# The input projection of a hybrid decoder block, whole and first, as seven block products per column pair

## The chip, the cores and the metric

One core of a Trainium2 chip runs the kernel. The metric is the device time of one execution in microseconds (us). Of the kernel before there are three timed runs, and one further execution that the hardware profiler recorded. The engines are named as the profile names them: PE is TensorE (PEld its weight loads), DVE is VectorE, ACT is ScalarE, POOL is GpSimd, SP is SyncE, which only issues DMAs here.

## What is computed

One layer over x of 1024 rows and 1024 columns, all in float32.

```python
u = rms_norm(h, mix_pre_g)
z = jnp.einsum('bsd,de->bse', u, w_in)      # 1024 x 4096
p, q, k, v = z[..., :o1], z[..., o1:o2], z[..., o2:o3], z[..., o3:o4]   # 512 columns each
gate_a, gate_b = z[..., o4:o5], z[..., o5:]                             # 1024 columns each
ya = jnp.einsum('bsc,cd->bsd', pool_mixer(p, pool_mix, pool_scale), w_branch_a)
yb = jnp.einsum('bsc,cd->bsd', diff_attention(q, k, v, ...), w_branch_b)
m = jax.nn.sigmoid(gate_a) * ya + jax.nn.sigmoid(gate_b) * yb
h = h + rms_norm(jnp.einsum('bsd,de->bse', m, w_out), mix_post_g)
u = rms_norm(h, ffn_pre_g)
f = jax.nn.silu(u @ w_ffn_gate) * (u @ w_ffn_up)
h = h + rms_norm(f @ w_ffn_down, ffn_post_g)
```

pool_mixer takes causal window means of 2, 4, 8 and 16 rows less the row itself, one window for each of four groups of 128 columns, and multiplies each group by its own 128 x 128 matrix. diff_attention has four heads with two 64-wide query and key parts each; a head's weights are the softmax of the first part less lambda times that of the second, with a linear distance bias and a causal mask.

## The kernel before

Every matrix product is made of float32r matmuls: each operand is split into a high part (a copy rounded to float32r, on ACT) and a low part (the rest, a subtraction on DVE), and three matmuls of 128 x 128 by 512 columns are summed: high by high, high by low, low by high. mac (line 103) does that for a plain product. Activations lie transposed, features on partitions.

The program is one traced function. A planner puts each engine's instructions in order from its own estimate of costs: among those whose inputs it holds to be ready, the earliest in program order goes first. Each engine then runs its queue strictly in that order, and so does each DMA queue. A pool of tiles is shared by tag: a8 has 16 buffers of 8 KB per partition, b4 has 14 of 4 KB, the weight tags wraw, whi and wlo have two of 4 KB each; in PSUM the tags mm, fil and pair have two buffers each (pair is two banks). A tile waits until a buffer of its tag is free. Code under tc.manual_schedule, or in tc.keep_in_program_order, keeps its written order on the engines named.

The stages, in program order:
- Start (first_block, line 208, and norm_steps, line 133): eight blocks of 128 rows of x are loaded, normed, transposed and split into uT (eight a8 buffers). Head 0's q and k products run in half-width pieces (proj_steps, line 190) as the blocks become ready.
- Attention (scores, transposes, values, from line 284): 32 blocks of four heads, in the order QORDER within a head, three in flight (AHEAD). Each block has scores on PE, a reduction on DVE that adds the bias and finds the row maximum, the exponential on ACT, a combination on DVE, transposes on PE, copies and subtractions (AT), the value matmuls on PE, and scalings on ACT and DVE. Beside it a filler generator is advanced by PACE steps for each attention step: head_proj (line 229) of the next head, the pool's projection (pool_windows, line 366) beside head 3.
- Pool mixing (from line 466), then the gated branches: gated (line 490) makes, for each of eight column blocks and two halves, the plain gate product (24 matmuls), the branch product (12 matmuls), the sigmoid on ACT and the multiplication on DVE; first for branch a, then for branch b with the transposed attention output (OT).
- Output projection and second norm (out_matmul, line 587), which keep the normed rows as quadrants of a two by two block matrix.
- FFN gate and up (gate_up, line 698): each pair of a gate and an up column block is a two by two block product, made with seven block products instead of eight: 7 x 4 x 3 = 84 matmuls for 96. ffn_weights builds the weight sums, sums and convert_u2 the activation sums S1 to S4.
- FFN down, also with seven products, operands through DRAM (fsd), and the last norm.

The projection of w_in has 32 column blocks of 128: four each for p, q, k and v, eight for each gate. Each costs 2 halves x 8 x 3 = 48 matmuls.

## Time and profile before

| | |
|---|---|
| median of three runs | 1319.32 us (1318.79 to 1319.73) |
| the profiled execution, its own time | 1322.02 us |
| span of the profiled execution, first to last instruction | 1320.2 us |
| mean granted TensorE clock in it | 0.996 |
| PE, DVE, ACT, POOL busy | 1292.2, 753.5, 528.9, 125.4 us |
| DMA | 128.81 MB, mean 98 GB/s |

The span is what the rows lie in; the execution's own time is 1.8 us longer, and 2.7 us above the median of the other runs. The busy time of an engine is the union of its instructions in a stretch. A matmul's duration runs from its start to its modelled end and overlaps the next one's, so the cost of a stream of matmuls is read from the distance of starts. A row of groups (by line) has the sum of one line's instructions, their mean in ns, and the engine's idle time just before them with what ended it.

### The profile page before, as it was taken

The page shows a single profiled execution, that of the slowest core. Times are in us where ns is not written, and L with a number is a line of the kernel's source. Part 1 is how long each engine was busy: PE and PEld are TensorE (multiplying, and loading weights), DVE is VectorE, ACT ScalarE, POOL GpSimd, SP SyncE. Part 2 cuts the span into 40 slices and gives each one's busy share as a digit, 9 for nine tenths or more (in the row PEclk, how much of TensorE's full clock was granted, in tenths as well). Part 3 has the DMA queues.
Part 4 walks back from the last instruction along what each step waited for, and adds up shares of the span by engine and source line. Part 5 has one row for each costly group of instructions (what it writes and reads, how often), then busy time and mean ns, then how long its engine had stood idle before and what let it go on. Part 6 is the DMA issues. An engine that isn't in the chain of part 4 may idle for free.

```text
span 1320.2 us, 15626 instructions
## 1 busy us (share of the span) xinstructions
PE 1292.2 (98%) x6024; PEld 1069.6 (81%) x6024; DVE 753.5 (57%) x1182; ACT 528.9 (40%) x967; POOL 125.4 (9%) x112
## 2 busy tenths in 40 slices
PE   5899999999999999999999999999999999999997
PEld 5788888887888788878878888888888888888886
DVE  5366676876111322255579756555655536874666
ACT  5256565545111211144455333333333324454552
POOL 4000000000000000001010111111101111000222
PEclk9899999999999999999999999999999999999999
DMA  6221212001111211143332323323232348833235
GB/s 211 65 53 44 65 33 64 9 25 40 44 45 44 78 48 48 48 144 112 116 124 71 110 99 120 120 97 104 88 112 95 105 165 284 276 105 103 88 104 199
DMA packets 123738, 128.81 MB, mean 98 GB/s; under 512 B 6288, under 2 KB 92816, under 8 KB 122256
## 3 DMA queue, kind: packets, MB, share of 16 engines
q1 hardware_dynamic: 120112, 121.39, 29.2%
q10 hardware_dynamic: 3552, 6.43, 1.3%
q8 instruction: 47, 0.77, 0.2%
q14 instruction: 27, 0.22, 0.0%
HBM read 95.03 MB, written 28.57 MB: 94 GB/s over the span
## 4 chain that ended last, share of the span: by engine, by line
PE 90%; DVE 4%; DMA 2%; ACT 1%; issue 1%; POOL 1%; SPq 0%; DVEq 0%; ACTq 0%; POOLq 0%
PE Y L688 6%; PE Y L689 6%; PE Y L687 6%; PE gate L109 4%; PE gate L111 4%; PE gate L110 4%; PE X L687 3%; PE X L689 3%; PE X L688 3%; PE o L344 3%; PE Yd L688 2%; PE Yd L689 2%; PE Yd L687 2%; PE branch L111 2%; PE branch L109 2%; PE branch L110 2%
## 5 line engine op out<-in xcount | busy, mean ns | idle before, releaser
L109 PE MATMUL gate<-uTh,wg_hi 128*128 128x512 f32 x256 | 101.5, 397 | 0.8 <-ACT p L376 0.4
L110 PE MATMUL gate<-uTl,wg_hi 128*128 128x512 f32 x256 | 101.3, 396 | 0.0
L111 PE MATMUL gate<-uTh,wg_lo 128*128 128x512 f32 x256 | 101.3, 396 | 0.0
L87 DVE TENSOR_TENSOR w_op<-wd,w_op 128x512 fp32r<-128x512 f32 x77 | 56.3, 731 | 50.1 <-ACT w_op L624 50.1
L624 ACT CAST w_op<-wd 128x512 fp32r<-128x512 f32 x77 | 47.9, 622 | 74.7 <-PE Yd L689 31.5
L629 DVE TENSOR_TENSOR p<-Z,p 128x512 f32<-128x512 f32 x21 | 14.5, 691 | 106.1 <-PE Z L689 106.1
L688 PE MATMUL Y<-A_lo,Wh 128*128 128x512 f32 x184 | 71.7, 390 | 0.3 <-DVE A_lo L87 0.3
L689 PE MATMUL Y<-A_hi,Wl 128*128 128x512 f32 x184 | 71.6, 389 | 0.0
L687 PE MATMUL Y<-A_hi,Wh 128*128 128x512 f32 x184 | 71.6, 389 | 0.0
L655 ACT CAST Wh<-wf_t 128x1024 fp32r<-128x1024 f32 x42 | 44.1, 1051 | 66.1 <-PE X L688 30.1
L127 POOL TENSOR_TENSOR rstd<-ms,mhalf 128x1 f32<-128x1 f32 (+1 forms) x11 | 11.7, 1064 | 603.7 <-DVE ms L126 587.5
L688 PE MATMUL Yd<-w_op,s_op 128*128 128x512 f32 x176 | 68.7, 390 | 0.2 <-DVE w_op L87 0.2
L687 PE MATMUL Yd<-w_op,s_op 128*128 128x512 f32 x176 | 68.6, 390 | 0.0
L689 PE MATMUL Yd<-w_op,s_op 128*128 128x512 f32 x176 | 68.3, 389 | 0.0
L309 ACT ACTIVATE E<-E,nm 128x1024 f32<-128x1024 f32 (+7 forms) x64 | 49.5, 774 | 40.3 <-DVE nm L306 39.8
L687 PE MATMUL X<-S_hi,Wh 128*128 128x512 f32 x168 | 65.4, 389 | 0.0
L688 PE MATMUL X<-S_lo,Wh 128*128 128x512 f32 x168 | 65.4, 389 | 0.0
L689 PE MATMUL X<-S_hi,Wl 128*128 128x512 f32 x168 | 65.4, 389 | 0.0
L687 PE MATMUL Y<-S_hi,Wh 128*128 128x512 f32 x168 | 65.4, 389 | 0.0
L688 PE MATMUL Y<-S_lo,Wh 128*128 128x512 f32 x168 | 65.4, 389 | 0.0
L689 PE MATMUL Y<-S_hi,Wl 128*128 128x512 f32 x168 | 65.4, 389 | 0.0
L87 DVE TENSOR_TENSOR wg_lo<-wg_raw,wg_hi 128x1024 fp32r<-128x1024 f32 x16 | 19.6, 1225 | 76.0 <-ACT wg_hi L101 76.0
(271 smaller groups left out, 3430.2 us busy)
## 6 DMA issues: line engine op xcount, KB each, us to landing
s_raw<-fsd SPq DMA_DIRECT2D x35, 512.0 KB, 3.6
wf_raw<-in_w_ffn_gate_dram SPq DMA_DIRECT2D x22, 512.0 KB, 3.7
wf_raw<-in_w_ffn_up_dram SPq DMA_DIRECT2D x22, 512.0 KB, 3.8
fsd<-fss SPq DMA_DIRECT2D x11, 1024.0 KB, 3.8
wd<-in_w_ffn_down_dram SPq DMA_DIRECT2D x44, 256.0 KB, 5.6
fsd<-F SPq DMA_DIRECT2D x33, 256.0 KB, 2.3
wg_raw<-in_w_in_dram SPq DMA_DIRECT2D x16, 512.0 KB, 3.9
xt<-in_x_dram SPq DMA_DIRECT2D x8, 512.0 KB, 8.1
```

The lines of the kernel that those rows point to most:

```text
L87: nc.vector.tensor_tensor(out=o, in0=a, in1=f32(hi), op=ALU.subtract)
L109: nc.tensor.matmul(o, ah, bh, start=i == 0, stop=False)
L110: nc.tensor.matmul(o, ah, bl, start=False, stop=False)
L111: nc.tensor.matmul(o, al, bh, start=False, stop=i == n - 1)
L309: nc.scalar.activation(E[m], E[m], AF.Exp, bias=nm[:, m:m + 1], scale=-1.0, accum_out=sums[:, m:m + 1])
L344: nc.tensor.matmul(o, ats[b // 4][:, j, b % 4 * P:(b % 4 + 1) * P], V[:, b, :, :], start=b == 0 and j == 0, stop=b == qb and j == 1)
L624: nc.scalar.copy(hi, a)
L629: nc.vector.tensor_tensor(out=o, in0=a, in1=b, op=op)
L655: nc.scalar.copy(hi, a)
L687: nc.tensor.matmul(o, ah, bh, start=start, stop=False, skip_group_check=goes_on)
L688: nc.tensor.matmul(o, ah, bl, start=False, stop=False, skip_group_check=goes_on)
L689: nc.tensor.matmul(o, al, bh, start=False, stop=stop, skip_group_check=goes_on)
```

## The change

The whole input projection comes first. Heads 0 and 1 have their q and k made plainly as before (common); the other 28 column blocks form 14 pairs, each made by seven block products in seven_steps, the routine that gate_up now shares: q with k of heads 2 and 3, v with a pool group (vp_unit, four of them), gate a with gate b (eight). The results go to DRAM: q and k in high and low parts (qkd), v transposed and split (vd), the pool branch's mixed output (yd), the sigmoids of the gates (sgd). load_head reads a head back into QA, QB, K and V.

The x norm runs in a written order on ACT, DVE and POOL, with the first weights' low parts on POOL; in its second half it also builds the raw sums for S1 to S4. The units follow. Of the last gate pair's 28 steps, 4 are taken before attention is begun, and the other 24 are the first of the filler. The filler then loads the pool output, head 1, and computes branch a (64 steps of three matmuls), with its weights' low parts on POOL instead of DVE. PACES sets the steps taken for each attention step: 2.2 for the first 9 steps, 0.5 for the next 10, then 0.3. Heads 2 and 3 are loaded during the head before. Branch b runs after attention. What follows (the output projection on) is the same work; some helpers have moved and been renamed.

```diff
 A8, B4 = 16, 14
-GROUPS = [2] * 9 + [4]
 QORDER = (7, 0, 6, 1, 5, 2, 4, 3)
-LAG, LAG_P = 4, 12
-PACE = (0.8, 0.8, 0.8, 0.7)
+LAG = 4
+PACES = (2.2, 0.5, 0.3, 0.3)
...
+    def load_w(src, k, n, s, pool=False):
 
         raw = wp.tile([P, k, n], F32, tag="wraw", bufs=2, name=name(s + "_raw"))
         hi = wp.tile([P, k, n], F32R, tag="whi", bufs=2, name=name(s + "_hi"))
         lo = wp.tile([P, k, n], F32R, tag="wlo", bufs=2, name=name(s + "_lo"))
         nc.sync.dma_start(raw, src.rearrange("(k p) n -> p k n", p=P))
-        if start:
-            tc.keep_in_program_order(nc.scalar.copy(hi, raw))
-            for i in range(0, k, 2):
-                tc.keep_in_program_order(nc.gpsimd.tensor_tensor(
-                    out=lo[:, i:i + 2, :], in0=raw[:, i:i + 2, :], in1=f32(hi[:, i:i + 2, :]), op=ALU.subtract))
+        nc.scalar.copy(hi, raw)
+        if pool:
+            nc.gpsimd.tensor_tensor(out=lo, in0=raw, in1=f32(hi), op=ALU.subtract)
         else:
-            nc.scalar.copy(hi, raw)
             sub(lo, raw, hi)
...
+        g, u = raw_weights(first, "wraw"), raw_weights(second, "whi")
+        operand(g, "B11", "B21")
+        t13, t24 = (wp.tile([P, 2, 4, P], F32, tag="wlo", bufs=2, name=name("wf_t")) for _ in range(2))
+        tt(t13[:, 0], u[:, 0], g[:, 0], ALU.subtract)
+        tt(t13[:, 1], u[:, 1], u[:, 0], ALU.subtract)
+        operand(t13, "T1", "T3")
+        tt(t24[:, 0], u[:, 1], t13[:, 0], ALU.subtract)
+        tt(t24[:, 1], g[:, 1], t24[:, 0], ALU.subtract)
+        operand(t24, "T2", "T4")
+        operand(u[:, 1:], "B22")
+        return W
...
+        yield from product_steps(Y, W["B11"], U["A11"], True)
+        p1 = temp("p1")
+        nc.scalar.copy(p1, Y)
+        yield from product_steps(X, W["T1"], U["S1"], True)
+        p5 = temp("p5")
+        nc.scalar.copy(p5, X)
+        yield from product_steps(Y, W["T2"], U["S2"], False)
+        u2 = temp("u2")
+        nc.scalar.copy(u2, Y)
+        yield from product_steps(Z, W["B21"], U["A12"], True)
+        add(Z, p1, 0, 0)
+        yield from product_steps(Y, W["T3"], U["S3"], False)
+        add(Y, p5, 1, 1)
+        yield from product_steps(X, W["B22"], U["S4"], False)
+        add(X, u2, 1, 0)
+        yield from product_steps(Y, W["T4"], U["A22"], False)
+        done(0, 1, Y)
...
+    U = {n: operand(n) for n in ("A11", "A12", "A21", "A22")}
+    traws = {n: a8([P, 4, HALF], F32, n + "_raw") for n in ("A11", "A12", "S1", "S3")}
+    traws["S2"], traws["S4"] = traws["A11"], traws["A12"]
...
+    qkd = [[dr.tile([P, 2, S], F32, name=name("qkd")) for _ in range(2)] for _ in range(NH)]
+    vd = [dr.tile([P, 2, S], F32, name=name("vd")) for _ in range(NH)]
+    yd = [dr.tile([P, 2, S], F32, name=name("yd")) for _ in range(4)]
+    sgd = [[dr.tile([P, S], F32, name=name("sgd")) for _ in range(KD)] for _ in range(2)]
...
+    def qk_done(h, e, t, src, st=None):
+        st = b4([P, 2, HALF], F32R, "qk_st") if st is None else st[e][:, :, half(t)]
+        hi, lo = st[:, 0], st[:, 1]
+        if e == 0:
+            qs = 1.0 / (8.0 * 0.25 ** (h + 1))
+            nc.scalar.mul(hi, src, qs)
+            nc.vector.scalar_tensor_tensor(out=lo, in0=src, scalar=qs, in1=f32(hi), op0=ALU.mult, op1=ALU.subtract)
+        else:
+            split((hi, lo), src)
+        nc.scalar.dma_start(qkd[h][e][:, :, half(t)], f32(st))
...
+    with tc.manual_schedule(engines={nc.scalar.engine, nc.vector.engine, nc.gpsimd.engine}):
+        for tb in range(2):
+            square(tb)
+            rstd(tb)
+        for tb in range(2):
+            normed(tb)
+        first_hi(0)
+        for part in range(4):
+            first_lo(0, part)
+        square(2)
+        rstd(2)
+        o = [(fil("q"), fil("k")), (mm("q"), mm("k"))]
+
+        def first_pair(i):
+            for e in range(2):
+                common(0, e, i // 2, o[i // 2][e], slice(i % 2 * 2 * P, (i % 2 + 1) * 2 * P))
+
+        for tb in range(NB):
+            t, cols = tb // 4, slice(tb % 4 * P, (tb % 4 + 1) * P)
+            both = pair("x_t")
+            for k in range(KD):
+                nc.tensor.transpose(both[:, k // 4, k % 4 * P:(k % 4 + 1) * P], xts[tb][:, k * P:(k + 1) * P], ident)
+            v = [both[:, kq, :].rearrange("p (k t) -> p k t", k=4) for kq in range(2)]
+            ops = [[a[:, :, cols] for a in U[f"A{t + 1}{kq + 1}"]] for kq in range(2)]
+            for kq in range(2):
+                nc.scalar.copy(ops[kq][0], v[kq])
+            if tb + 3 < NB:
+                square(tb + 3)
+            if tb in (0, 2, 4):
+                first_hi(tb // 2 + 1)
+            for kq in range(2):
+                sub(ops[kq][1], v[kq], ops[kq][0])
+            if tb + 2 < NB:
+                normed(tb + 2)
+            if tb + 3 < NB:
+                rstd(tb + 3)
+            if tb < 6:
+                for part in range(2):
+                    first_lo(tb // 2 + 1, part + tb % 2 * 2)
+            if t == 0:
+                for kq in range(2):
+                    nc.scalar.copy(traws[f"A1{kq + 1}"][:, :, cols], v[kq])
+            else:
+                s1, s2, s3, s4 = (traws[f"S{i + 1}"][:, :, cols] for i in range(4))
+                nc.scalar.copy(s1, v[0])
+                tt(s1, v[1], s1, ALU.add)
+                tt(s2, s1, s2, ALU.subtract)
+                tt(s3, v[1], s2, ALU.subtract)
+                tt(s4, s4, s2, ALU.subtract)
+            if tb + 5 < NB:
+                xts.append(load_x(tb + 5))
+            if tb < 2:
+                first_raw(tb + 2)
+            if tb in (3, 5, 7):
+                first_pair(tb // 2 - 1)
+            if tb == 7:
+                for e in range(2):
+                    qk_done(0, e, 0, o[0][e])
+    first_pair(3)
+    for e in range(2):
+        qk_done(0, e, 1, o[1][e])
+    W = weights(w_cols(o_q, 2), w_cols(o_k, 2))
+    for t in range(2):
+        o = (fil("q"), fil("k")) if t == 0 else (mm("q"), mm("k"))
+        for e in range(2):
+            common(1, e, t, o[e], slice(0, HALF))
+            qk_done(1, e, t, o[e])
+    for n in ("S1", "S2", "S3", "S4"):
+        U[n] = operand(n)
+        split(U[n], traws[n])
...
+    def vp_unit(h):
+
+        VS = a8([P, 2, S], F32R, "v_st")
+        v = VS.rearrange("p i (b d) -> p b i d", b=NB)
+        pp = a8([P, 2, S], F32, "p")
+        p, seen = pp[:, 0, :], [0, 0]
+
+        def done(e, t, src):
+            seen[e] += 1
+            if e == 0:
+                if t == 1:
+                    vt = temp("vt")
+                    nc.scalar.copy(vt, src)
+                    src = vt
+                pt = fil("vT")
+                for i in range(4):
+                    nc.tensor.transpose(pt[:, i * P:(i + 1) * P], src[:, i * P:(i + 1) * P], ident)
+                pt = pt.rearrange("p (b d) -> p b d", b=4)
+                split((v[:, t * 4:t * 4 + 4, 0, :], v[:, t * 4:t * 4 + 4, 1, :]), pt)
+                if seen[e] == 2:
+                    nc.scalar.dma_start(vd[h], f32(VS))
+            elif seen[e] == 2:
+                later.append(lambda: pool(h, p, pp[:, 1, :]))
+
+        unit(w_cols(o_v, h), w_cols(0, h), done, lambda e, t: p[:, half(t)] if e == 1 else None)
...
+        tmp = [s0, b4([P, S], F32, "s")]
+        win = WINDOWS[g]
+        s, w, i = p, 1, 0
+        while w < win:
+            s2 = tmp[i]
+            nc.vector.tensor_copy(s2[:, :w], s[:, :w])
+            tt(s2[:, w:], s[:, w:], s[:, :S - w], ALU.add)
+            s, w, i = s2, 2 * w, 1 - i
+        tt(s[:, :16], s[:, :16], cnt[:, g, :], ALU.mult)
+        tt(p[:, :16], s[:, :16], p[:, :16], ALU.subtract)
+        nc.vector.scalar_tensor_tensor(out=p[:, 16:], in0=s[:, 16:], scalar=1.0 / win, in1=p[:, 16:],
+                                       op0=ALU.mult, op1=ALU.subtract)
+        y = b4([P, S], F32R, "yh"), b4([P, S], F32R, "yl")
+        split(y, p)
+        o = pair("y")
+        for t in range(2):
+            mac(o[:, t, :], [((pm[:, 0], pm[:, 1]), tuple(a[:, half(t)] for a in y))])
+        o = o.rearrange("p t c -> p (t c)")
+        y2 = b4([P, S], F32R, "y2h"), b4([P, S], F32R, "y2l")
+        nc.scalar.mul(y2[0], o, psc[:, g:g + 1])
+        nc.vector.scalar_tensor_tensor(out=y2[1], in0=o, scalar=psc[:, g:g + 1], in1=f32(y2[0]),
+                                       op0=ALU.mult, op1=ALU.subtract)
+        for i in range(2):
+            nc.scalar.dma_start(yd[g][:, i, :], f32(y2[i]))
...
+    def gate_done(d):
+        st, seen = [b4([P, S], F32, "g_st") for _ in range(2)], [0, 0]
+
+        def done(e, t, src):
+            nc.scalar.activation(st[e][:, half(t)], src, AF.Sigmoid)
+            seen[e] += 1
+            if seen[e] == 2:
+                nc.scalar.dma_start(sgd[e][d], st[e])
+        return done
+
+    def unit(first, second, done, where=lambda e, t: None, W=None):
+        W = W or weights(first, second)
+        while later:
+            later.pop(0)()
+        seven(W, U, done, where)
+
+    for h in range(2, NH):
+        unit(w_cols(o_q, h), w_cols(o_k, h),
+             W=W if h == 2 else None, done=partial(qk_done, h, st=[a8([P, 2, S], F32R, "qk_st") for _ in range(2)]))
+    for h in reversed(range(NH)):
+        vp_unit(h)
...
+    def load_head(h):
+
+        QA, K = (a8([P, 2, S], F32R, n) for n in ("QA", "K"))
+        for m in range(2):
+            r, r2 = hs[m], hs[1 - m]
+            nc.sync.dma_start(f32(K[r, m, :]), qkd[h][1][r, 0, :])
+            nc.sync.dma_start(f32(K[r2, m, :]), qkd[h][1][r, 1, :])
+            for rr in (r, r2):
+                nc.sync.dma_start(f32(QA[rr, m, :]), qkd[h][0][r, 0, :])
         yield
+        QB, V = (a8([P, 2, S], F32R, n) for n in ("QB", "V"))
+        for m in range(2):
+            for rr in hs:
+                nc.sync.dma_start(f32(QB[rr, m, :]), qkd[h][0][hs[m], 1, :])
+        nc.sync.dma_start(f32(V), vd[h])
+        heads[h] = QA, QB, K, V.rearrange("p i (b d) -> p b i d", b=NB)
+
+    head0 = load_head(0)
+    for d in range(KD - 1):
+        if d == 3:
+            next(head0)
+        unit(w_cols(o_ga, d), w_cols(o_gb, d), gate_done(d))
+
+    last_unit = seven_steps(weights(w_cols(o_ga, KD - 1), w_cols(o_gb, KD - 1)), U, gate_done(KD - 1))
+    for _ in range(4):
+        next(last_unit)
+    for _ in head0:
+        pass
...
+    def branch(e, w, mov, take):
+
+        for d in range(KD):
+            bh, bl = load_w(w[:, d * P:(d + 1) * P], 4, P, "wb", e == 0)
+            for t in range(2):
+                sg = temp(("p1", "sg")[t])
+                nc.sync.dma_start(sg, sgd[e][d][:, half(t)])
+                o = fil("branch")
+                for k in range(4):
+                    triple(o, bh[:, k, :], bl[:, k, :], *mov(t, k), k == 0, k == 3, False)
+                    yield
+                take(d, t, o, sg)
...
+    def filling():
+        yield from last_unit
+        for i in range(2):
+            y2.append((a8([P, 2, S], F32R, "y2h"), a8([P, 2, S], F32R, "y2l")))
+            for j in range(2):
+                for t, s in zip(y2[i], range(2)):
+                    nc.sync.dma_start(f32(t[:, j, :]), yd[2 * i + j][:, s, :])
+        ma.extend([[a8([P, 4, HALF], F32, "ma") for _ in range(KD // 4)] for _ in range(2)])
+        for _ in load_head(1):
+            pass
+        yield from branch(0, w_branch_a, quad_mov(y2), take_a)
+
+    filler = filling()
...
-            owed += pace
-            while filler is not None and owed >= 1.0:
+            owed += PACES[min(steps // 10, len(PACES) - 1)]
+            while owed >= 1.0:
                 owed -= 1.0
-                if next(filler, True):
-                    owed = -1e9
+                next(filler, None)
...
+            if pos == 2 and 0 < h < NH - 1:
+                for _ in load_head(h + 1):
+                    pass
             step(scores(*seq[j]))
```

## Rows read from the trace of the kernel before

**Rows 1.** Page, part 1: busy us, share of the span, instructions.

```profile
PE 1292.2 (98%) x6024; PEld 1069.6 (81%) x6024; DVE 753.5 (57%) x1182; ACT 528.9 (40%) x967; POOL 125.4 (9%) x112
```

**Rows 2.** Busy time by stretch: attention, gated branches, FFN gate and up.

```profile
core 0: us, PE busy (x) PEld busy (x) DVE busy (x) ACT busy (x) POOL busy (x), PEclk, DMA share, GB/s
76.90:297.00 220.10, 220.10 (x1199) 188.96 (x1198) 160.08 (x363) 123.15 (x308) 5.96 (x3) 1.00 0.16 41
316.00:582.70 266.70, 266.70 (x1161) 214.65 (x1160) 73.08 (x94) 54.64 (x79) 0.00 (x0) 1.00 0.19 57
706.10:1086.90 380.80, 380.80 (x1681) 315.31 (x1680) 227.26 (x264) 134.58 (x181) 63.11 (x41) 1.00 0.33 108
```

**Rows 3.** ACT in order of time: start, us, what; first copy of two FFN units.

```profile
744.23 0.59 ACT L707 COPY p<-Y 128x512 f32<-128x512 f32 x1 [1.44 <-issue]
763.26 0.59 ACT L707 COPY p<-Y 128x512 f32<-128x512 f32 x1 [1.45 <-issue]
```

**Rows 4.** ACT in order of time: sigmoids of two gate column blocks, one half.

```profile
480.03 0.59 ACT L501 ACTIVATE sg<-gate 128x512 f32<-128x512 f32 x1
496.83 0.59 ACT L501 ACTIVATE sg<-gate 128x512 f32<-128x512 f32 x1
```

**Rows 5.** Start, in order of time: one x block's norm, copy, square, subtractions.

```profile
20.80 1.28 DVE L140 SCALAR_TENSOR_TENSOR xt<-xt,rstd,g 128x1024 f32<-128x1024 f32 x1 [1.25 <-POOL rstd L138]
21.38 0.59 ACT L155 CAST uTh<-x_t 128x512 fp32r<-128x512 f32 x1 [0.69 <-PE x_t L148]
21.86 1.06 ACT L136 ACTIVATE junk<-xt 128x1024 bf16<-128x1024 f32 x1
22.00 1.28 DVE L156 TENSOR_TENSOR uTl<-x_t,uTh 128x512 fp32r<-128x512 f32 x2
```

**Rows 6.** Busy time by stretch, as rows 2: a stretch of the FFN down projection.

```profile
1122.00:1155.00 33.00, 33.00 (x147) 27.35 (x146) 28.86 (x49) 15.69 (x30) 0.00 (x0) 1.00 0.86 279
```

**Rows 7.** PE's groups in 76.9 to 297: values, first and last projection line.

```profile
L344 PE MATMUL o<-V,AT 128*128 128x256 f32 x264 | 38.2, 285 | 0.0
...
L198 PE MATMUL p<-uTh,wp_hi 128*128 128x512 f32 x62 | 24.8, 401 | 0.0
...
L198 PE MATMUL q<-uTh,wq_hi 128*128 128x512 f32 x40 | 15.8, 396 | 0.0
```

**Rows 8.** DVE's groups in 52 to 316: attention lines, first three and last.

```profile
L306 DVE CUSTOM_DVE_ANT_0 E<-s,negd 128x1024 f32<-128x1024 f32 (+7 forms) x64 | 47.1, 751 | 16.3 <-PE s L303 16.3
L87 DVE TENSOR_TENSOR AT<-aT,AT 128x512 fp32r<-128x512 f32 (+3 forms) x48 | 26.0, 551 | 5.4 <-ACT AT L332 5.1
L315 DVE SCALAR_TENSOR_TENSOR E<-E,cf,E 128x1024 f32<-128x1024 f32 (+3 forms) x16 | 17.2, 1077 | 0.1
...
L360 DVE TENSOR_TENSOR O<-O,rstd 128x1024 f32<-128x1024 f32 x4 | 4.9, 1220 | 4.7 <-POOL rstd L127 4.7
```

**Rows 9.** DVE in order of time: two adjoining instructions.

```profile
183.20 1.21 DVE L306 CUSTOM_DVE_ANT_0 E<-s,negd 128x1024 f32<-128x1024 f32 x1
184.34 0.08 DVE L306 DVE_READ_ACCUMULATOR2_ANT nm<- 128x1 f32 x1
```

**Rows 10.** Busy time by stretch, as rows 2: attention's densest 30 us.

```profile
232.00:262.00 30.00, 30.00 (x170) 25.73 (x169) 25.10 (x59) 18.11 (x49) 2.66 (x1) 1.00 0.03 10
```

**Rows 11.** PE in order of time: first matmul of the output projection.

```profile
582.70 0.40 PE L582 MATMUL wo<-woh,mh 128*128 128x512 f32 x1
```

**Rows 12.** Start, in order of time: a subtraction on POOL beside a norm.

```profile
16.48 2.40 POOL L98 TENSOR_TENSOR w_lo<-w_raw,w_hi 128x256 fp32r<-128x256 f32 x2
16.55 1.74 DVE L140 SCALAR_TENSOR_TENSOR xt<-xt,rstd,g 128x1024 f32<-128x1024 f32 x1 [1.35 <-POOL rstd L138]
```

**Rows 13.** Busy time by stretch, as rows 2: a spell at the low clock.

```profile
55.00:60.00 5.00, 5.00 (x13) 3.90 (x12) 0.69 (x1) 0.13 (x1) 0.00 (x0) 0.50 0.44 131
60.00:65.00 5.00, 5.00 (x23) 4.02 (x22) 0.00 (x0) 0.59 (x1) 0.00 (x0) 0.99 0.00 0
```

**Rows 14.** PE in order of time: two matmuls after idle gaps, ahead of that.

```profile
51.91 0.47 PE L302 MATMUL s<-K,QA 128*128 128x512 f32 x1 [1.11 <-ACT wq_hi L101]
53.95 0.77 PE L198 MATMUL v<-uTh,wv_hi 128*128 128x512 f32 x1 [1.56 <-DVE QB L252]
```

More of the change, by code (lines that the diff above doesn't have):

```diff
@@ new lines, in raw_weights, with weights, operand @@
+    def raw_weights(src, tag):
+        r = wp.tile([P, 2, 4, P], F32, tag=tag, bufs=2, name=name("w_raw"))
+        nc.sync.dma_start(r.rearrange("p h k n -> p (h k) n"), src.rearrange("(k p) n -> p k n", p=P))
+        return r
+    def weights(first, second):
+        W = {}
+        def operand(a, *names):
+            for _ in weight_operand(W, a, *names):
+                pass
[10 more added lines that the diff above has]
+        return W
@@ new lines, in common, with square, rstd, normed @@
+    def common(h, e, t, o, c):
+        _, hi, lo = plain[h, e]
+        mac(o[:, c], [((hi[:, k, :], lo[:, k, :]),
+                       tuple(a[:, k % 4, c] for a in U[f"A{t + 1}{k // 4 + 1}"])) for k in range(KD)])
+    def square(tb):
+        ss = small(1, "ss")
+        sumsq(xts[tb], ss)
+        xr.append(ss)
+    def rstd(tb):
+        xr[tb] = rstd_of(xr[tb], 1, D)
+    def normed(tb):
+        nc.vector.scalar_tensor_tensor(out=xts[tb], in0=xts[tb], scalar=xr[tb], in1=g1, op0=ALU.mult, op1=ALU.mult)
@@ L422, in block_kernel @@
+    filler = filling()
     seq = [(h, qb) for h in range(NH) for qb in QORDER]
     AHEAD = 2
-    filler, pace, owed, steps, late = None, 0.0, 0.0, 0, []
+    owed, steps, late = 0.0, 0, []
     def defer(n, f):
@@ L520, in block_kernel, with take_b @@
                                            op1=ALU.subtract)
-    gated(o_gb, w_branch_b, quad_mov(OT), False)
+    def take_b(d, t, o, sg):
+        md = m[t][d // 2][:, d % 2, :]
+        tt(md, o, sg, ALU.mult)
+        tt(md, md, ma[t][d // 4][:, d % 4, :], ALU.add)
+    for _ in branch(1, w_branch_b, quad_mov(OT), take_b):
+        pass
     wo = []
@@ L881, in operands, with down_block @@
         return so, wo
[L883 removed]
+    def down_block(o, so, wo, tb, kb, new):
         c = slice(tb * P, (tb + 1) * P)
```

437 lines of the change are left out of this document (146 added, 291 removed).

## The prediction

> **What bounds the kernel now.** I read the page's busy shares first, then the stages in a table of stretches, then TensorE's rows inside each stage. TensorE is busy for 98% of the span [rows 1], and in the three long stages this change touches or copies (attention, the gated branches, the gate and up projections) it is busy for the whole stretch, while VectorE has 160 of 220 us, 73 of 267 us and 227 of 381 us [rows 2]. So the bound is the number of matmuls times their spacing. The duration column (390 ns) is not the spacing, since matmuls overlap; the spacing comes from a periodic event. One seven-product unit of the FFN (84 matmuls) repeats every 19.03 us, 0.2266 us a matmul [rows 3]. One gate column block with its branch (72 matmuls) repeats every 16.80 us, 0.2333 us a matmul [rows 4].
>
> **Part 1: seven products for eight.** A pair of column blocks costs 96 matmuls now, 96 x 0.2333 = 22.4 us, and 84 x 0.2266 = 19.03 us afterwards. 28 of the 32 column blocks of w_in go into 14 pairs (q and k of heads 0 and 1 stay plain), so TensorE loses 14 x 3.37 = 47 us of work. This is the whole gain. Its other work stays: x transposes, scores, values, both branches, pool mixing.
> The unit's VectorE load is that of an FFN unit, 227.26 / 20 = 11.4 us of 19 [rows 2]. The four v/p units add the pool windows: about seven 1024-column operations for window 16 at 1.28 us each (estimate from the norm operation of that width [rows 5]), and the V splits. That is near 21 us of VectorE work in a unit which with its transposes and pool matmuls lasts 21.3 us, less for the smaller windows. I take 1 us lost in each, 4 us; the bounds are 0 and, if each pool chain had to end before the next unit's weights find a buffer, 10 us each.
> The stores (qkd, vd, yd, sgd, 24 MB) are issued on ACT behind the low-part subtraction on VectorE, so ACT's next copy (p1, p5 of the following product) queues behind that wait. ACT has 134.58 / 20 = 6.7 us of work in 19 [rows 2]: costed at nothing, 1 us a unit if that cover is gone. The 28 MB read back are issued on SP behind and ahead of the weight loads. 52 MB over some 560 us is 93 GB/s more; a stretch with 279 GB/s had TensorE busy throughout [rows 6]. Costed at nothing. The head loads replace 32 SBUF-to-SBUF copies on the same queue.
>
> **Part 2: the start.** ACT, VectorE and GpSimd now follow a written order over the eight x blocks. ACT has per block two copies (0.59 each), a square (1.06 and its read) and one or two further copies for the raw operands; VectorE has two subtractions (1.28 together), the norm (1.28) and, in the second half, four more 512-column sums at about 0.64 [rows 5]. That is about 4 us a block on ACT for blocks 0 to 3 and 3.8 to 5.1 us on VectorE for blocks 4 to 7, against about 3.2 us now. Starting at 14 us, I get the last low part at 49 us instead of 38. Behind it TensorE still has the last pair of head 0 (48 half-width matmuls, 5.7 us) and head 1 (96 x 0.2266 = 21.8 us), which cover the S operands and the first weights. First unit: 49 + 5.7 + 21.8 + 2.5 for a spell at the low clock = 79 us. Bounds 73 and 87.
> The units: 79 + 13 x 19.03 + one product of the last unit (2.7) + V transposes (3.5) + pool matmuls (24 x 0.2333 = 5.6) + the 4 us above = 342 us.
>
> **Part 3: attention with less to fill it.** Until now 624 projection matmuls fill TensorE beside attention. Afterwards there are 72 left from the last unit and 192 of branch a. TensorE's own attention work: in the fully busy 220.1 us, 596 projection matmuls take 139 us, V transposes 3, which leaves 78 us for 264 of the 288 value matmuls, so 85 us for all [rows 2, 7]. With 72 + 162 filler matmuls (54 of the 64 branch steps by PACES) it is 139 us, some 11 us of it done before the first score. So VectorE takes over as the bound. Its attention lines (nine, from 47.1 us down to 4.9 us) sum to 134 us [rows 8]; adjoining instructions overlap by 0.07 us [rows 9], about half of some 310, so 123 us. The change adds the branch multiplies in attention (13 x 0.64 = 8.6), 2 for the last unit, and 4 for GpSimd in the way (next paragraph): 138 us. ACT is below that at some 110.
> How full VectorE gets there is the unknown that decides. Nearest row: in the densest 30 us of this stage it is 84% busy while TensorE is the bound [rows 10]; the other end is 100%. I take 88%, near the row: 157 us. At 100% it is 138, at today's stage average of 73% [rows 2] it is 190.
> The first score needs QB and V, whose buffers are those of A11, free after the last unit's first product. 2 MB at 279 GB/s [rows 6] is 7.5 us, with landing 9: first score at 351 us, while TensorE runs the other 24 triples. Attention ends at 351 + 157 = 508. Ten filler triples (7 us) then cover the last head's norm, to 515. O transposes 3.5 and branch b 192 x 0.2333 = 44.8 follow: 563 us. SP's sg loads wait for their two buffers, and the branch weights and the next head's loads queue behind them; the head loads have a third of a head's time in hand, so I cost this at nothing (5 us if not). The first matmul of the out projection stands at 582.7 us now [rows 11], and from there on the program is the same. Sum: 563 - 582.7 = -19 us.
>
> **Two rules weighed.** Branch a's low parts move to GpSimd. One VectorE norm beside a GpSimd subtraction took 1.74 us where others take 1.28 [rows 5, 12]; eight such operations of twice the width cost about 4 us. The Trainium skill (SBUF — State Buffer, Who interferes with whom) says that the two share a port pair held for a whole instruction. That speaks against the change, and the slow row agrees with it; if every one of the eight held VectorE up for its whole length, 15 us, the sum would be -7.
> TensorE fell to 0.50 of its clock, the 1.2 GHz level, after two idle gaps of 1.1 and 1.6 us with one matmul between them: 13 matmuls in 5 us against 23 [rows 13]. The gaps are there in the order of its matmuls [rows 14]. The Trainium skill (TensorE: Matmul & The Clock Gate, Why this matters for your kernels) warns of idle gaps between bursts as what drops the clock; it names longer ones than these rows show. By that rule the clock would hold in attention, and by the rows it may not, which is the third rival.
>
> **The rivals.**
> One, attention packs perfectly: VectorE at 100%, 138 us, another 19 us off: 1281. For it: three blocks are in flight and branch work is independent. Against: each block passes PE, VectorE, ACT, VectorE, PE, ACT, VectorE, PE, ACT, VectorE in fixed queue orders.
> Two, slower: that chain, not VectorE's sum, sets the pace, and the share stays at 73%: 190 us, 33 us more, net +14: 1333. It turns from gain to loss at 176 us of attention (78%). For it: reductions and reciprocals wait on PE and ACT even now. Against: now they wait because TensorE's filler stands in front.
> Three, slower: TensorE drops to its low level in attention, where it is only 80% busy. Each us of its work costs one more there; about 30 us of slack absorb as much, so low for half of the 128 us it adds some 34 us: 1334.
> Four, buffers: U holds 14 of the 16 large buffers during the units, so v_st and p are single, and the pool's six small ones fill the 14. If each v/p unit waits 10 us for its predecessor: 36 us more, 1336. Against: the vd store ends some 8 us into the next unit, which writes V only after its fourth product (11 us).
> Five, the change does less than it says: the units run at the gates' 0.2333 us: 14 x 84 x 0.0067 = 8 us less, 1308. The trace doesn't say why the two spacings differ; both FFN and new units keep weights in the same tag, so I hold to 0.2266.
>
> **How the numbers follow.** The profiled execution has a span of 1320.2 us, and its own time of 1322.0 is 2.7 above the median 1319.3; the sum is a difference and is taken from the median: 1300. Forecast with case five (1288 to 1314): 0.48. One: 0.17. Two: 0.20, spread from 1312 upwards. Three: 0.07. Four: 0.08. About 0.2% is what a measurement of this kernel can tell from no change. Faster: 0.48 + 0.17 + 0.05 of the others = 0.70; same 0.09; slower 0.21. Range 1281 to 1329: it reaches case one and most of two, leaving out the rest of two to four.
>
> **What would show it.** Right: units 19.0 us apart, the first near 79 us, first score near 351, VectorE at 85 to 92% and TensorE near 80% in attention, first out matmul near 563. Wrong: VectorE idle behind ACT and PE in turn in attention (two), a granted clock of 0.5 there (three), gaps between v/p units ended by a pool line or a DMA (four), units 19.6 us apart (five). The forecast fails first on VectorE's share in attention: each 5 points there are about 9 us.

## The result and the profile after

The changed kernel takes 1307.82 us (median of four, 1307.38 to 1311.67), the kernel before 1319.2 us: a ratio of 0.992, 95% interval 0.990 to 0.994, so 11.4 us less. The forecast was 19 us less. The profiled execution is the longest of the four (1311.67 us, span 1309.9, mean granted clock 0.985); the other three are about 4 us shorter (clock 0.991 to 0.992).

The page of the kernel after: busy time by engine (against [rows 1]), the granted clock in 40 slices, and the shares of the chain that ended last.

```profile
PE 1262.0 (96%) x5856; PEld 1046.0 (80%) x5856; DVE 837.4 (64%) x1301; ACT 578.6 (44%) x1031; POOL 141.2 (11%) x128
...
PEclk8899999999999998999999999999999999999999
...
PE 83%; DVE 7%; DMA 3%; ACT 3%; issue 2%; POOL 1%; ACTq 0%; SPq 0%; DVEq 0%; POOLq 0%
```

TensorE is busy 30 us less and stands idle 48 us instead of 28; the span fell by 10.3. Where the idle time lies, by stretch (columns as in [rows 2]): the 14 units, attention, O transposes with branch b, output projection.

```profile
82.00:344.00 262.00, 260.87 (x1160) 214.01 (x1159) 148.32 (x200) 108.31 (x154) 2.50 (x2) 1.00 0.39 132
344.00:517.10 173.10, 160.09 (x889) 135.77 (x888) 130.51 (x331) 110.24 (x292) 17.24 (x12) 0.95 0.55 164
517.10:568.20 51.10, 49.70 (x227) 39.04 (x227) 32.93 (x49) 13.43 (x23) 1.64 (x1) 1.00 0.41 133
568.20:667.70 99.50, 97.03 (x439) 78.48 (x438) 57.32 (x89) 46.70 (x92) 8.96 (x14) 0.98 0.37 128
```

The units are full (260.87 of 262.00). Attention is not: TensorE 92%, at 0.95 of its clock, VectorE 130.51 of 173.10, which is 75%. Cut in three, the stage is uneven:

```profile
344.00:380.00 36.00, 35.34 (x182) 28.71 (x181) 17.97 (x44) 26.00 (x47) 2.96 (x3) 1.00 0.97 300
380.00:500.00 120.00, 110.47 (x642) 94.76 (x641) 101.38 (x257) 74.41 (x216) 14.28 (x9) 0.97 0.50 146
500.00:517.10 17.10, 14.28 (x70) 12.30 (x69) 11.16 (x31) 9.82 (x30) 0.00 (x0) 0.70 0.00 1
```

VectorE is busy for 50% of the ramp, where TensorE still runs the last unit's products; for 84% of the middle; for 65% of the drain, where TensorE has nothing but attention left and its granted clock is 0.70 in the mean.

The times that the forecast named are in these rows, ACT and PE in order of time: the first unit's copy (first product's end 2.7 us after the unit's start), two gate units' copies as in [rows 3], the first score matmul that needs QB, the last value products, and the output projection's first matmul [rows 11].

```profile
84.66 0.59 ACT L266 COPY p<-Y 128x512 f32<-128x512 f32 x1 [1.19 <-PE Y L232]
268.06 0.59 ACT L266 COPY p<-Y 128x512 f32<-128x512 f32 x1 [1.10 <-PE Y L232]
287.10 0.59 ACT L266 COPY p<-Y 128x512 f32<-128x512 f32 x1 [1.10 <-PE Y L232]
...
349.42 0.47 PE L612 MATMUL s<-K,QB 128*128 128x512 f32 x1 [0.25 <-DMA QB<-qkd]
513.31 4.04 PE L653 MATMUL o<-V,AT 128*128 128x256 f32 x18
568.17 0.39 PE L793 MATMUL wo<-woh,mh 128*128 128x512 f32 x1
```

What VectorE, and then ScalarE, waited for in attention (us in total, times, longest us; 344 to 517):

```profile
DVE rec L622 <- ACT E L618: 16.2, 21, 3.2
DVE E L615 <- PE s L612: 10.4, 5, 6.2
DVE O L659 <- ACT O L658: 7.4, 11, 1.4
DVE AT L86 <- ACT AT L641: 3.2, 5, 1.2
...
ACT O L658 <- PE o L653: 19.9, 17, 2.1
ACT E L618 <- DVE nm L615: 19.3, 26, 1.2
ACT junk L127 <- DVE O L659: 9.9, 16, 1.3
```

VectorE waits for ScalarE's exponentials and ScalarE for VectorE's row minima: each is idle behind the other in turn, as the second rival described it.

### The profile page after: what moved, and what is told of

Same layout as the page of the kernel before. It is cut to its first block, busy times and chain, and to the rows that moved or that the text cites. A ratio compares the mean times of both kernels' runs of the same rounds, so it can differ in the third digit from the quotient of the medians.

```text
span 1309.9 us, 15669 instructions
## 1 busy us (share of the span) xinstructions
PE 1262.0 (96%) x5856; PEld 1046.0 (80%) x5856; DVE 837.4 (64%) x1301; ACT 578.6 (44%) x1031; POOL 141.2 (11%) x128
## 3 DMA queue, kind: packets, MB, share of 16 engines
q1 hardware_dynamic: 127776, 146.56, 35.4%
## 4 chain that ended last, share of the span: by engine, by line
PE 83%; DVE 7%; DMA 3%; ACT 3%; issue 2%; POOL 1%; ACTq 0%; SPq 0%; DVEq 0%; POOLq 0%
PE Y L230 9%; PE Y L232 9%; PE Y L231 9%; PE X L230 5%; PE X L231 5%; PE X L232 5%; PE Yd L231 3%; PE Yd L230 2%; PE Yd L232 2%; PE Z L230 2%; PE Z L232 2%; PE Z L231 2%; PE o L653 2%; PE wo L794 2%; PE wo L795 2%
## 5 line engine op out<-in xcount | busy, mean ns | idle before, releaser
L231 PE MATMUL Y<-A_lo,Wh 128*128 128x512 f32 x296 | 115.7, 391 | 0.3 <-DVE A_lo L86 0.3
L230 PE MATMUL Y<-A_hi,Wh 128*128 128x512 f32 x296 | 115.3, 390 | 0.0
L230 PE MATMUL X<-S_hi,Wh 128*128 128x512 f32 x280 | 109.1, 390 | 0.1
L230 PE MATMUL Y<-S_hi,Wh 128*128 128x512 f32 x280 | 109.2, 390 | 0.0
L86 DVE TENSOR_TENSOR Wl<-wf_t,Wh 128x1024 fp32r<-128x1024 f32 x70 | 86.6, 1244 | 4.7 <-ACT Wh L199 4.7
L199 ACT CAST Wh<-w_raw 128x1024 fp32r<-128x1024 f32 x72 | 60.4, 841 | 63.1 <-PE Z L231 41.9
L86 DVE TENSOR_TENSOR Wl<-w_raw,Wh 128x1024 fp32r<-128x1024 f32 x72 | 69.6, 966 | 14.4 <-ACT Wh L199 14.4
L159 DVE TENSOR_TENSOR wf_t<-w_raw,wf_t 128x512 f32<-128x512 f32 x70 | 65.7, 939 | 1.0
L231 PEld LDWEIGHTS Y<-A_lo,Wh 128*128 128x128 f32 x296 | 55.6, 188 | 12.1 <-DVE A_lo L86 0.7
L232 PEld LDWEIGHTS Y<-A_hi,Wl 128*128 128x128 f32 x296 | 55.6, 188 | 11.4
```

Source lines behind the costliest of these rows:

```text
L86: nc.vector.tensor_tensor(out=o, in0=a, in1=f32(hi), op=ALU.subtract)
L159: nc.vector.tensor_tensor(out=o, in0=a, in1=b, op=op)
L199: nc.scalar.copy(hi, a)
L230: nc.tensor.matmul(o, ah, bh, start=start, stop=False, skip_group_check=goes_on)
L231: nc.tensor.matmul(o, ah, bl, start=False, stop=False, skip_group_check=goes_on)
L232: nc.tensor.matmul(o, al, bh, start=False, stop=stop, skip_group_check=goes_on)
```

## The experiments

Theories of the 167.7 us from QB's score at 349.4 to the last value product. **A:** VectorE's sum of work sets the pace, so a microsecond of it costs a microsecond. **B:** the chain through the engines does, with only two attention blocks started ahead; then VectorE's work counts in part, and more blocks in flight shorten the stage. **C:** the missing filler on TensorE does. Besides these, the runs measure the start, the sevens and the output projection by themselves.

"Stage" is the time from the first score matmul to the last value product. The three kernels whose attention code is the same (the changed one and two of the runs below) show 172.1 to 173.4 us for it, while whole executions of one kernel differ by some 5 us. So stages are compared, one trace each, and totals only where several rounds were run. In the changed kernel the stage is 173.1.

**VectorE more.** 32 extra 512-column sums on VectorE, one for each attention block.

```diff
         attends[h, qb] = E[0], rec
+        tt(spare, negd[:, :HALF], negd[:, HALF:], ALU.add)
```

> One more 512-column sum on VectorE per attention block (32 of them, about 0.66 us each, 21 us; nobody waits for its result). Stage from first score to last value: 173 us in the changed kernel. Theory A, VectorE's sum of work sets the pace of attention (the forecast's): 173 grows by 17 to 21 us. Theory B, the fixed chain through the engines sets it and VectorE's 25% idle time is waiting: it grows by 3 to 9 us. Theory C, TensorE's filler sets it: 0 to 5 us.

Measured: VectorE's busy time in the stage rose by 20.1 us, the stage by 5.5 (178.6); total 1315.74. A quarter of the added work came through: against A.

**VectorE less.** The transposed weights' low part isn't computed, and the values use the high part twice (so the result lacks that correction); TensorE and ScalarE do the same work.

```diff
-            sub(AT[:, 1, :n * P], pt[:, :n * P], AT[:, 0, :n * P])
...
-                nc.tensor.matmul(o, ats[b // 4][:, j, b % 4 * P:(b % 4 + 1) * P], V[:, b, :, :],
+                nc.tensor.matmul(o, ats[b // 4][:, 0, b % 4 * P:(b % 4 + 1) * P], V[:, b, :, :],
```

> The low part of the attention weights AT is left out and the high part used twice, so 48 subtractions (26 us) leave VectorE and one link leaves each block's chain, while TensorE has as many matmuls as before. Theory A: the stage of 173 us shrinks by 18 to 24 us. Theory B: by 10 to 20 us, with VectorE's share no higher than now. Theory C, TensorE's filler sets it: by 0 to 5 us.

Measured: 22.7 us less on VectorE (130.5 to 107.8), 15.3 us less of stage, total 1293.56. Stretches of the two kernels, more and less:

```profile
344.00:522.60 178.60, 159.81 (x888) 136.98 (x887) 150.58 (x363) 110.22 (x290) 16.36 (x12) 0.94 0.53 159
...
342.10:499.90 157.80, 151.70 (x888) 127.24 (x887) 107.78 (x283) 109.95 (x290) 16.50 (x12) 1.00 0.60 179
```

The removed operation stood in the chain, between transposes and values; the added one stood beside it. With less work VectorE is not fuller but emptier, 68%. That is B: an operation costs by its place in the chain. The clock, 1.00 instead of 0.95, has a share in the 15.3 that this run doesn't separate.

**TensorE more, TensorE less.** The first matmul of each of branch a's 16 products issued four more times (64 extra matmuls); and branch a without the product with its weights' low part (64 fewer, the branch result lacks that part).

```diff
+                for _ in range(4 if e == 0 else 0):
+                    nc.tensor.matmul(o, bh[:, 0, :], mov(t, 0)[0], start=True, stop=False, ...)
```

```diff
-                    triple(o, bh[:, k, :], bl[:, k, :], *mov(t, k), k == 0, k == 3, False)
+                    if e == 0:
...
+                        nc.tensor.matmul(o, bh[:, k, :], ah, start=k == 0, stop=False)
+                        nc.tensor.matmul(o, bh[:, k, :], al, start=False, stop=k == 3)
...
```

> Four more matmuls per column block and half of branch a (64, about 14.7 us of TensorE beside attention; the first matmul of each product issued five times). Theory A and B: the stage of 173 us grows by 0 to 5 us, less if TensorE's clock falls less often. Theory C: by 10 to 15 us.

> Branch a leaves out the product of the high weights' remainder (its low-part weights), 64 matmuls, 14.7 us of TensorE less beside attention. Theory A and B: the stage of 173 us changes by -3 to +3 us, or grows where TensorE's clock falls more often. Theory C: it shrinks by 10 to 15 us.

Measured: 64 matmuls more, stage 169.9 (3.2 shorter), total 1306.88; 64 fewer, stage 171.3 (1.8 shorter), total 1307.59. Stretches, more and less:

```profile
344.40:514.30 169.90, 164.60 (x953) 140.83 (x952) 130.24 (x331) 111.11 (x292) 16.75 (x12) 1.00 0.56 166
...
342.00:513.30 171.30, 146.63 (x825) 122.94 (x823) 129.90 (x331) 111.10 (x290) 17.16 (x12) 0.96 0.55 165
```

Some 15 us of TensorE work either way (64 x 0.23) moves the stage by 3 at most, and added work doesn't lengthen it. C falls. TensorE's 92% in the changed kernel isn't the bound either: with 64 matmuls fewer it is 86%, and the stage is nearly as long. That added work shortened it goes with the clock, 1.00 for 0.95.

**Warm matmuls in the drain.** Eight unread 256-column matmuls behind the values of head 3's last five blocks, to hold the clock up there.

```diff
+        if h == NH - 1 and qb in QORDER[3:]:
+            w = fil("warm")
+            for j in range(8):
+                nc.tensor.matmul(w[:, :2 * P], ats[0][:, 0, :P], V[:, j, :, :], start=True, stop=True)
```

> Eight extra half-width matmuls, which nobody reads, behind the value products of each of the last five blocks of head 3 (40 of them, 4.7 us of TensorE at the full clock). Theory clock: the last 17 us of attention lose 3 to 5 us to TensorE's low level (granted 0.83 and 0.51 there); with the extra work the level holds and the stage from first score to last value goes from 173 to 168 to 170 us. Rival, chain alone: the extra matmuls stand in the way, 173 to 177 us.

Measured: 1314.27 us. The drain (500 to 512.9) ran at clock 1.00 and the stage was 170.9, 2.2 shorter, but the planner moved the work about: some 29 of branch a's matmuls now run behind attention (the last at 520.5 instead of 490.2), and last value to first out matmul is 58 instead of 51. Inconclusive: the shorter stage also has less in it.

**Three blocks ahead.** Nothing but the order changes: scores of three blocks instead of two are started ahead of the oldest's transposes.

```diff
-    AHEAD = 2
+    AHEAD = 3
...
-        j = i + AHEAD - 1
+        j = i + 1
```

> Scores are issued three blocks ahead of the value products instead of two. Theory B (chain through the engines with too few blocks in flight): the stage of 173 us shrinks by 5 to 15 us, VectorE's share rises above 78%. Rival, the buffers (14 small tiles, two PSUM pairs) or the planner's fixed order already bound the blocks in flight: -2 to +10 us.

Measured: stage 164.4, 8.7 shorter, total 1303.24. The same ramp and middle as above:

```profile
343.30:380.00 36.70, 34.02 (x167) 27.16 (x166) 17.97 (x46) 25.83 (x45) 4.26 (x4) 1.00 0.97 302
380.00:500.00 120.00, 115.44 (x690) 99.38 (x691) 108.32 (x277) 81.64 (x234) 11.84 (x8) 0.99 0.48 139
...
DVE rec L622 <- ACT E L618: 10.2, 15, 3.1
```

VectorE does the same 17.97 us in the ramp and 7 us more in the middle (90% busy); its wait for the exponentials (last row) fell from 16.2 to 10.2 us. The clock in the stage is 0.98 instead of 0.95, which may have given a part (the next run bounds it).

**Four blocks ahead** (AHEAD = 4, with the same second line):

> The changed kernel with scores four blocks ahead. If the chain needs still more blocks in flight the stage goes below the 164 us that three ahead gave; if the 14 small tiles (two for a long block's E, two for its AT, O and the bias beside them) are the limit by now, 162 to 172 us.

Measured: stage 160.2, 12.9 shorter, total 1297.59 (one run). Ramp, middle and drain:

```profile
343.90:380.00 36.10, 33.85 (x165) 26.89 (x163) 17.01 (x43) 27.48 (x45) 3.33 (x4) 1.00 0.96 308
380.00:490.00 110.00, 105.07 (x648) 92.03 (x648) 101.70 (x265) 76.21 (x223) 13.09 (x9) 1.00 0.51 147
490.00:504.10 14.10, 12.10 (x77) 10.23 (x76) 10.31 (x26) 8.60 (x26) 0.00 (x0) 1.00 0.25 76
```

The middle is now 92% VectorE, the drain 73%, and the ramp is as empty as before: what is left there isn't a matter of blocks in flight. The clock is 1.00 in all three stretches, but it doesn't make the gain by itself: the run with more TensorE work had 1.00 too, and with two blocks ahead its stage was 169.9. By that run some 3 of the 12.9 us can be the clock's.

**Three blocks ahead in the kernel before.** The same edit, where 624 projection matmuls still lie beside attention.

> The kernel before with scores three blocks ahead instead of two, and nothing else. Theory B says that the chain's waits matter only where TensorE has too little beside them: in the kernel before TensorE is busy throughout attention, so no change, 1316 to 1323. Rival, three ahead is better by itself, whatever fills TensorE: 5 us or more faster.

Measured: 1319.63 us beside 1320.35 for the kernel before, and TensorE busy for 219.14 of the 220.1 us of [rows 2]'s first stretch:

```profile
76.90:297.00 220.10, 219.14 (x1187) 187.13 (x1186) 160.49 (x361) 123.07 (x305) 4.93 (x3) 1.00 0.16 41
```

There the chain's latency was covered by filler and more blocks gain nothing. The runs with three and four blocks ahead and this one together show B.

**Eight products instead of seven,** the rest of the change kept.

```diff
-        W = W or weights(first, second)
+        W = W or eight_weights(first, second)
...
-        seven(W, U, done, where)
+        for _ in eight_steps(W, done, where):
+            pass
```

Here a unit multiplies its two column blocks of weights by both halves of x in eight plain block products of 12 matmuls.

> The changed kernel with eight block products (96 matmuls) in each of its 14 units instead of seven; the S operands are not split. The gain of part 1 alone. If the matmuls keep the units' spacing of 0.2267 us, units come 21.8 us apart instead of 19.04, the units' stretch grows by 13 x 2.72 = 35 us and the whole by 33 to 39 us, to about 1344. If plain products run at the gates' 0.2333 us, units come 22.4 us apart and the whole grows by 42 to 48 us. Rival, the units were bound by VectorE or DMA and not by matmuls: under 25 us.

Measured: 1341.18 us (one run). ACT in order of time, the same step of two gate units:

```profile
249.39 0.63 ACT L530 ACTIVATE g_st<-p 128x512 f32<-128x512 f32 x1
271.15 0.63 ACT L530 ACTIVATE g_st<-p 128x512 f32<-128x512 f32 x1
```

21.76 us for 96 matmuls, 0.2267 each, the spacing of the sevens. PE in order of time, the first matmul of the first unit, in the changed kernel and with eight products:

```profile
81.74 0.39 PE L230 MATMUL Y<-A_hi,Wh 128*128 128x512 f32 x1
...
78.49 0.39 PE L230 MATMUL Y<-A_hi,Wh 128*128 128x512 f32 x1
```

From there to the first score are 262.3 us (to 344.0) and 297.9 us (to 376.4): 35.6 us more, as 13 x 2.72 = 35.4 asks. The units start 3.3 us earlier there, where no S operands are split; so in the whole the sevens are worth 33 us, and without them the change is a loss of 21 us.

**Column sums out of the start's written order.** The sums S1 to S4 are made as wide operations ahead of their splits, not within each x block.

```diff
-                tt(s1, v[1], s1, ALU.add)
-                tt(s2, s1, s2, ALU.subtract)
-                tt(s3, v[1], s2, ALU.subtract)
-                tt(s4, s4, s2, ALU.subtract)
+                nc.scalar.copy(s3, v[1])
```

> The 16 column sums for S1 to S4 leave the written order of the x norm and are made behind it, as four wide operations ahead of each split. The first unit starts at 82 us in the changed kernel, 3 later than forecast. Theory, VectorE's sums in blocks 4 to 7 delay the low parts that TensorE waits for: the first unit starts 3 to 6 us earlier, at 76 to 79. Rival, VectorE is nearly full from 55 to 75 us as well and the sums then delay the S operands: the unit starts or is held at 82 to 87 us.

Measured: first unit's copy at 79.44 us, against 82.6 to 85.0 in the nine kernels that keep this start: 3 to 6 us earlier. Total 1303.72 (one run).

**The output projection's weights earlier,** inside branch b (step 4 of every 8) instead of behind it.

```diff
+    for i, _ in enumerate(branch(1, w_branch_b, quad_mov(OT), take_b)):
+        if i % 8 == 4:
+            load_wo(i // 8)
```

> The eight loads and splits of w_out are written into branch b, one behind each column block, instead of behind all of it. Theory late weights: the changed kernel loses about 4 us behind attention (output projection's first to last matmul 99.5 us against 95.6 in the kernel before) since w_out arrives late and the gap drops TensorE to 0.66 of its clock; here that stage takes 95 to 96 us and the whole is 3 to 5 us shorter than the changed kernel's 1307.8, about 1303.5. Rival, the gap belongs to the m operands of the last column block or to something else: no change, 1307 to 1309.

Measured: 1307.07 us (four runs, 1305.96 to 1307.75), ratio 0.990 [0.989, 0.992], not told apart from the changed kernel's 0.992; the 3 to 5 us expected of the whole don't show in it. The output projection shows the effect: first to last out matmul 94.8 us instead of 99.5, while last value to first out matmul is 52.8 instead of 51.1. The first two rows are the changed kernel's, the last two the edit's:

```profile
570.00:575.00 5.00, 3.37 (x14) 2.18 (x12) 4.96 (x10) 3.32 (x6) 0.00 (x0) 1.00 0.39 123
575.00:580.00 5.00, 5.00 (x16) 3.96 (x15) 2.41 (x4) 1.05 (x1) 0.00 (x0) 0.66 0.59 206
...
570.00:575.00 5.00, 5.00 (x23) 4.01 (x22) 1.68 (x5) 0.00 (x0) 0.00 (x0) 1.00 0.00 0
575.00:580.00 5.00, 5.00 (x23) 4.04 (x22) 0.00 (x0) 0.43 (x2) 0.00 (x0) 1.00 0.00 0
```

**Three together:** AHEAD = 3, sums later, weights earlier.

> Three blocks ahead, the column sums behind the x norm, and w_out loaded inside branch b, together. By the single runs' stages the first unit starts 3 us earlier, attention is 9 us shorter and the stretch from the last value product to the output projection's last matmul 3 us shorter: 15 us in all if they add, 1307.8 - 15 = 1293. If the earlier attention end only meets w_out later, or the shorter attention lets TensorE's clock fall, 1297 to 1302.

Measured: 1295.64 us (five runs, 1292.88 to 1298.0), ratio to the kernel before 0.981 [0.980, 0.983]. This beats both kernels: 25 us under the kernel before, 12 under the changed one. Its stage is 165.1, its first unit's copy at 78.74, its out projection 94.6. The 15 us that the single runs add up to came out as 12. Four blocks ahead with the other two edits wasn't run.

## Why the prediction came out as it did

The forecast was 1300 in a range of 1281 to 1329; sign and range hold, and the gain is 8 us smaller than forecast. The profiled span fell by 10.3 against 19.3 (the -19 before rounding), so some 9 us have to be found. Term by term, as the prediction put them:

**Seven products: right in mechanism, its parts mixed.** The units come 19.04 us apart (268.06 to 287.10), as forecast, so rival five is false. The 47 us were 38 for the product count (14 x 12 x 0.2267) and 9 for the spacing, 0.2333 to 0.2266. The eight-product run shows that plain products in this layout have the shorter spacing too, so the 9 us belong to the new layout and not to the sevens. By the units' stretch the sevens give 35.6 us.

**The start: 3 us short.** First unit at 82 (84.66 - 2.72), forecast 79. In the nine kernels with this start the first matmul of the first unit falls into two groups: 79.7 to 79.9 in four, where the granted clock from 50 to 60 us was 1.00, and 81.1 to 82.1 in five, where it was below that (0.78 and 0.88 in the two halves in the changed kernel). So some 2 us go with a second spell at the low clock, where the forecast had one. TensorE is idle for 2.3 of the 5 us before 55, mostly behind VectorE's low parts; with the column sums out of the order it is idle for none of them, and the unit starts 3 to 6 us earlier.

**The four v/p units: 3 us lost, forecast 4.** The five copies stand at 122.74, 142.88, 165.19, 186.75 and 210.29: 87.6 us for four intervals, against 4 x 19.04 + 3.5 + 5.6 = 85.3, and the next interval is 0.6 longer than 19.04. Rival four (10 us each) is false. The last unit's first product ends at 344, forecast 342; the first score that needs QB is at 349.4, forecast 351: the loads were faster than costed, 5.4 us instead of 9.

**Attention: the step that was mis-sized.** Forecast 157 us from QB's score on, measured 167.7. Three corrections add up to it. VectorE's work was 130.25 us, not 138: at 88% that is 148.0, 9 less. (Its lines sum to 147.4 us, so adjoining instructions overlap by 17 us where the prediction took 11, and the 4 us for GpSimd weren't VectorE's.) The share in the middle was 84.5% (101.38 / 120), not 88%: 154.2 us, 6.2 more. And the share was taken for the whole stage, while ramp and drain run far below it: at 84.5% their VectorE work, 17.7 us from 349.4 to 380 and 11.16 behind 500, would take 34.2 us, and it took 47.7, 13.5 more. Sum: 157 - 9 + 6.2 + 13.5 = 167.7. The row taken as nearest [rows 10] was a good guess for the middle, and the wrong one for the ends. In the ramp TensorE is full (35.34 of 36.00) with the last unit's products and the DMA share is 0.97; ScalarE also changes its function table seven times there, since the last unit's sigmoids (L513) alternate with exponentials (L618). ACT in order of time, two of the seven:

```profile
356.22 1.28 ACT L513 ACT_TABLE_LOAD   x1
...
358.16 1.28 ACT L618 ACT_TABLE_LOAD   x1
```

Which of the three holds the ramp wasn't tried apart. Two of the forecast's own signs failed in this stage: VectorE at 85 to 92%, and TensorE near 80%, which is 92%. Of the latter some 7 us are the ten branch steps that the forecast put behind attention, and a part is the clock of 0.95; the rest isn't taken apart.

**Rival two was the mechanism, at a smaller size.** It put VectorE's share at 73%; from QB's score on it is 78% (130.25 / 167.7; 75% of the whole stage). That the change still gains is in part luck: on the 138 us of work that the prediction summed, this share would give 178 us, past its break-even of 176. What the prediction held against this rival, that VectorE waits because filler stands in front, fits the kernel before, where more blocks ahead gain nothing. The step from there to a VectorE that no longer waits once the filler is gone is what failed: with less filler it waits for the chain.

**Rival three: in part.** "TensorE drops to its low level": the drain ran at 0.70, the rows from 510 on at 0.51, the stage at 0.95. TensorE stood idle there for 2.8 of 17.1 us, in waits of at most 2 us for VectorE, gaps of the size of [rows 14]. What it cost isn't settled; the run with more TensorE work and clock 1.00 had a stage 3.2 us shorter, which points to a few us and not the rival's 34.

**GpSimd in the way: right resource, wrong victim.** The forecast charged VectorE 4 us for branch a's low parts. In attention it was GpSimd that was held, in order of time:

```profile
408.11 1.22 DVE L669 TENSOR_TENSOR O<-O,rstd 128x1024 f32<-128x1024 f32 x1
408.17 2.30 POOL L96 TENSOR_TENSOR wb_lo<-wb_raw,wb_hi 128x512 fp32r<-128x512 f32 x1 [0.47 <-ACT E L618]
...
449.49 1.29 POOL L96 TENSOR_TENSOR wb_lo<-wb_raw,wb_hi 128x512 fp32r<-128x512 f32 x1 [3.75 <-ACT wb_hi L94]
```

GpSimd takes 2.30 us instead of 1.29 where VectorE has begun first (three of the eight subtractions take 1.86 to 2.30 us, the others 1.29 or 1.30), and VectorE's wide E is as long as before (1078 ns against 1077 [rows 8]). In [rows 12] GpSimd had begun first, and VectorE paid: 1.74 us for 1.28. If the second one waits for the whole of the first, the subtraction above ends at 408.11 + 1.22 + 1.29 = 410.62; it ended at 410.47. The Trainium skill (SBUF — State Buffer, Who interferes with whom) calls the shared port pair an exclusive lock; both cases agree with that, and the price falls on the one that comes second. Eight subtractions of 1.29 us are 10 us, so the 15 us that the prediction took for its worst case were too many as well.

**Behind attention: 51.1 us, forecast 55.** The planner pulled branch a forward (its last matmul is at 490.2), so the ten leftover steps weren't behind attention, and the drain had no filler.

**"From there on the program is the same": false by 4 us.** The output projection takes 99.5 us where it took 95.6 (97.2 to 100.4 in the ten kernels that load its weights behind branch b). The weights pass through two raw buffers, which they share with branch b's weights, and a load waits until the split before it has freed one. SP in order of time, and the longest of these loads' waits from 515 to 585 us (wol is the low part, split on VectorE):

```profile
552.95 0.33 SPq L752 DMA_DIRECT2D wo_raw<-in_w_out_dram  x1
559.70 1.54 SPq L752 DMA_DIRECT2D wo_raw<-in_w_out_dram  x2
565.57 0.33 SPq L752 DMA_DIRECT2D wo_raw<-in_w_out_dram  x1
...
SPq L752 <- DVE wol L86: 12.3, 6, 3.0
```

The eight loads are issued from 552.95 to 580.4, the first out matmul is at 568.17; in the kernel before they went from 565.4 to 587.6, with the first out matmul at 582.7. So the last load now stands 12 us behind the first out matmul instead of 5. TensorE waits for the split weights, runs dry at 570 to 575 (3.37 of 5), and the clock is at 0.66 in the next 5 us. Issued earlier, the loads give 94.8 us. The prediction costed SP's waits for the head loads only, and at nothing; the loads behind branch b weren't on its list. Why the eight take 27 us instead of 22 isn't shown.

Sum against the forecast's span: +3 (start) - 1 (units) - 4 (score) + 11 (attention) - 4 (behind) + 4 (out projection) = +9.

## What to carry to other kernels

Work that fills an engine beside a latency-bound stage hides that stage's chain; when it moves elsewhere, look at how many blocks are in flight first, as the same two-line edit made the stage 8.7 us shorter here and gained nothing in the kernel before. Do not apply one busy share to a whole stage: ramp and drain have shares of their own, and each wants its own row. And where a stage gets shorter, ask what the next stage loads, from which queue, and whether it still comes in time.

## What the hardware showed that was not expected

TensorE can finish a stage earlier with more to do: 64 added matmuls, 15 us of work, went with a granted clock of 1.00 instead of 0.95 and a stage 3.2 us shorter. The three kernels with the same attention code fit this (173.1 and 173.4 us at 0.95, 172.1 at 0.97). That the clock is the cause is likely and not shown: each is one trace, and the run with spare matmuls in the drain also moved other work.

The spacing of 512-column matmuls is 0.2267 us in the units, with seven products or eight, and 0.2333 in the gates before [rows 4]; branch b, which keeps its old tiles, has 0.2325 in the changed kernel (36 triples from 541.67 to 566.78). It goes with the layout of the operands, weights and activations both, and not with the number of products; which part of the layout makes it isn't shown.
